# Six weight chunks rounded and split by DMAs, and one more projection in 512-wide pairs

## The chip, the cores and the metric

The kernel runs on one core of a Trainium2 chip. The metric is the device time of one execution in microseconds; the kernel before takes 251.93 us (median of three runs, 251.75 to 252.18). The engines are TensorE (PE for its matmuls, PEld for its weight loads), VectorE (DVE), ScalarE (ACT), GpSimd (POOL) and SyncE (SP). Each engine works through its own instructions in their order and waits on semaphores. SP issues almost all loads; in the kernel before, POOL issues none.

## The reference

Two decoder layers on x of 256 rows by 1024 (one batch). Each layer normalises x, projects it to 3584 columns, runs three branches over the pieces, gates them, and adds an output projection to x:

```python
hn = rms_norm(x, norm_gain)
proj = jnp.einsum('bsd,de->bse', hn, w_in)                      # 1024 -> 3584
a_q, a_k, a_v, a_g, b_x, b_g, c_q, c_k, c_v, c_g = jnp.split(proj, ...)
y_a = dilated_attention(rope(a_q), rope(a_k), a_v) * silu(a_g)  # 8 heads of 64
y_b = rg_lru_branch(b_x, ...) * silu(b_g)                       # 256 wide
y_c = stick_breaking_attention(c_q, c_k, c_v) * silu(c_g)       # 4 heads of 64
return x + jnp.einsum('bse,ed->bsd', concat(y_a, y_b, y_c), w_out)
```

A last RMSNorm follows the second layer. All inputs and the output are float32.

## The kernel before

**Precision.** Matmuls take float32r, a rounded float32. To keep float32 accuracy each operand is held twice: a rounded part `hi` and the rest `lo` = original - `hi`. A product is three matmuls: hi x hi, hi x lo and lo x hi. For the activations the parts are `xh` and `xl` (both in `xx`), or `yh` and `yl`.

**Weights** are packed in 18 chunks a layer, each 128 x 2048: 0 and 1 (`CH_AV`), 2 (`CH_CV`), 3 `CH_CQ`, 4 `CH_CK`, 5 and 8 `CH_AQ`, 6 and 9 `CH_AK`, 7 `CH_BX`, 10 `CH_CG` (C's gate), 11 `CH_BG`, 12 and 13 `CH_AG`, 14 to 17 the output projection. The second half of A's heads uses 8 and 9, called AQ1 and AK1 below; 5 and 6 are AQ0 and AK0. `load_chunk` (L101) fetches a chunk in two halves of 128 x 1024 into a staging tile `st` (five buffers) by a DMA on SP; ACT copies each 512 columns into `whi` (float32r, so the copy rounds), and DVE writes `wlo` = `st` - `whi`. `whi` and `wlo` have four buffers each, taken in rotation, so chunk n can be written only when TensorE is through with chunk n - 4. `ask` and `weights` (L117, L123) ask for a chunk two ahead of its use.

**A projection** of a 256-wide chunk is `proj_b` (L313), in two halves b = 0 and 1 of 128 columns. Unpaired (L340) a half is 24 matmuls 256 wide: `hi` with `xh`, `hi` with `xl`, `lo` with `xh`, eight k-blocks each, into half a PSUM bank. Paired (L323 to L338, chunks in `PAIRED[l]`) `hi` meets `xh` and `xl` at once: seven matmuls 512 wide, eight 256 wide for `lo`, and one more 512 wide, into one bank of its own for each half; ACT then copies the `xl` part out (`low`, L334) and DVE adds the two (L336, L338). Layer 0 pairs nothing; layer 1 pairs 3 to 9. Tag `pp` has three PSUM banks in rotation, so a half must wait until the bank of three before it has been read out.

**Order.** TensorE's order is the order in which the code is written. In a layer: V chunks, CQ, CK, AQ0 half 0, the stick-breaking scores (`sb_scores`, L434), AQ0 half 1, AK0, BX half 0, one block of transposes of the stick-breaking weights `sw` (`turned`, L460), BX half 1, two more blocks, AQ1 half 0, then `second` (the values `y` from the turned weights `wv`, L425, and A's first scores), AQ1 half 1, AK1, CG, transposes, BG half 0, `third` (gates, values, scores), BG half 1, AG, the output projection. The other engines' instructions are put in order by the framework's scheduler when the program is built. On ACT the sigmoids of `sb_scores` (L450, L451) feed DVE's scans (L456) and products (L458), whose result `sw` the transposes turn; ACT copies the turned blocks to `wv` (L466).

Of the kernel before, what the change touches and what calls it, by code (L numbers as in the profile page):

```python
# [9 lines left out]
F32 = mybir.dt.float32  # L10
F32R = mybir.dt.float32r
BF16 = mybir.dt.bfloat16
AF = mybir.ActivationFunctionType
ALU = mybir.AluOpType

P = 128
# [25 lines left out]

CH_AV, CH_CV, CH_CQ, CH_CK, CH_BX, CH_CG, CH_BG, CH_AG, CH_O = 0, 2, 3, 4, 7, 10, 11, 12, 14
CH_AQ, CH_AK = (5, 8), (6, 9)
PAIRED = ((), (CH_CQ, CH_CK, CH_AQ[0], CH_AK[0], CH_BX, CH_AQ[1], CH_AK[1]))


@with_exitstack
def trunk_kernel(ctx: ExitStack, tc: tile.TileContext, x, first_x, first, wpack, prm_d, gatew, gains, consts, rope, out):
    nc = tc.nc  # L50
    act, dve, pe, gps = nc.scalar, nc.vector, nc.tensor, nc.gpsimd
# [3 lines left out]
    wsp = ctx.enter_context(tc.tile_pool(name="wsp", bufs=4))  # L55
# [43 lines left out]
    split = {}  # L99

    def load_chunk(l, c):  # L101
        hi = wsp.tile([P, 2048], F32R, name="whi", tag="whi")
        lo = wsp.tile([P, 2048], F32R, name="wlo", tag="wlo")
        for i in range(2):
            st = wst.tile([P, 1024], F32, name="st", tag="st")
            nc.sync.dma_start(out=st, in_=wpack[l, c][:, i * 1024:(i + 1) * 1024])
            for j in range(0, 1024, 512):
                ws, ss = slice(i * 1024 + j, i * 1024 + j + 512), slice(j, j + 512)
                split[l, c] = act.activation(hi[:, ws], st[:, ss], AF.Copy)  # L109
                dve.tensor_sub(lo[:, ws], st[:, ss], hi[:, ws].bitcast(F32))  # L110
        return hi, lo
# [5 lines left out]
    def ask(l, c, ahead=AHEAD):  # L117
        last = order.index((l, c)) + ahead
        while pending and order.index(pending[0]) <= last:
            i = pending.pop(0)  # L120
            ready[i] = load_chunk(*i)

    def weights(l, c, ahead=AHEAD):  # L123
        ask(l, c, ahead)
        return ready.pop((l, c))
# [16 lines left out]
    for k in range(NK):  # L142
# [8 lines left out]
        hi, lo = [a[:, o:o + 768] for a in pair]  # L151
# [21 lines left out]
    prm_t = cst.tile([P, L * SM_P], F32, name="prm_t")  # L173
    nc.sync.dma_start(out=prm_t, in_=prm_d)
    ready[pending.pop(0)] = load_chunk(0, CH_CQ)
    xres = cst.tile([P, NT, D], F32, name="xres")
    for t in range(NT):
# [122 lines left out]
    for l in range(L):  # L300
# [12 lines left out]
        def proj_b(c, mid=None, to=None, sc=1.0):  # L313
            pair = c in PAIRED[l]
            hi, lo = [a.rearrange("p (k c) -> p k c", c=256) for a in weights(l, c, AHEAD - 1 if mid else AHEAD)]
            if pair:
                flat = None if to is not None else scr(512)
                to = v2(flat) if to is None else to
            else:
                flat = bank(pp, "pp")  # L320
            for b in range(2):
                cs = slice(b * P, b * P + P)
                if pair:  # L323
                    ps = bank(pp, "pp")
                    seq = [(0, k) for k in range(NK - 1)] + [(1, k) for k in range(NK)] + [(0, NK - 1)]
                    for i, (is_lo, k) in enumerate(seq):
                        if is_lo:
                            pe.matmul(ps[:, 0:S], lo[:, k, cs], xh[:, k, :], start=False, stop=False,  # L328
                                      skip_group_check=True)
                        else:  # L330
                            pe.matmul(ps, hi[:, k, cs], xx[:, k].rearrange("p h t -> p (h t)"), start=i == 0,  # L331
                                      stop=i == len(seq) - 1, skip_group_check=True)
                    low = wk.tile([P, S], F32, name="low", tag="low", bufs=2)
                    act.activation(low, ps[:, S:2 * S], AF.Copy, scale=sc)  # L334
                    if sc == 1.0:
                        dve.tensor_add(to[:, b, :], ps[:, 0:S], low)  # L336
                    else:
                        dve.scalar_tensor_tensor(to[:, b, :], ps[:, 0:S], sc, low, ALU.mult, ALU.add)  # L338
                else:
                    mm3(flat[:, b * 256:(b + 1) * 256], [lambda k, a=a: a[:, k, cs] for a in (hi, lo)],  # L340
                        [lambda k, a=a: a[:, k, :] for a in (xh, xl)], range(NK), True, True)
                if b == 0 and mid:
                    mid()
                    ask(l, c)
            return flat

        def proj_to(dst, c, mid=None, sc=1.0):
            if l > 0 and c in PAIRED[l]:
                proj_b(c, mid, dst, sc)
            else:  # L350
                scaled(dst, proj_b(c, mid), sc)
# [296 lines left out]
        for t in range(NT):  # L648
# [3 lines left out]
            for n2 in range(2):  # L652
                cs = slice(n2 * 512, n2 * 512 + 512)
# [5 lines left out]
                for c0, c1 in parts:  # L659
                    c = slice(n2 * 512 + c0, n2 * 512 + c1)  # L660
# [110 lines left out]
```

## Time and profile before

| | us |
|---|---|
| median of three runs (lowest, highest) | 251.93 (251.75, 252.18) |
| the profiled execution's own time | 251.52 |
| its span, first to last instruction | 249.4 |
| TensorE matmuls busy | 241.0 |
| DVE busy | 196.6 |
| ACT busy | 166.9 |
| POOL busy | 9.4 |
| read from HBM | 42.03 MB |

The span is what the profile's times are counted in; 2.1 us of the profiled execution lie around it. The granted TensorE clock was 0.997 over the span. A row of the timeline gives the start, the duration, the engine, the line, the operation and, in brackets, how long the engine sat idle before it and what released it; merged rows have a count. A row of the groups gives the count, the busy sum and the mean of one in ns, and the idle time before them. In the window rows the last three numbers are the granted clock, the busy share of the 16 DMA engines and the GB/s that they moved.

### The profile page before, as it was taken

The numbers are of one execution on the slowest core, as the hardware profiler recorded it, in microseconds if no ns is written. First come the engines' busy times: TensorE is split into PE (matmuls) and PEld (weight loads), VectorE is DVE, ScalarE is ACT, GpSimd is POOL, SyncE is SP. The second block draws the span as 40 slices with busy tenths as digits, with TensorE's granted clock in tenths as the row PEclk, the third lists the DMA queues.
The fourth block names the chain that finished last, engine by engine and source line by source line (L and its number), as shares of the span: only waits on it lengthen the run. The fifth ranks groups of instructions, "written<-read, shape, count | busy, mean of one in ns | idle before, by whom it ended". The sixth has DMA issues, their size and how long they took to land.

```text
span 249.4 us, 4520 instructions
## 1 busy us (share of the span) xinstructions
PE 241.0 (97%) x1657; PEld 214.7 (86%) x1657; DVE 196.6 (79%) x445; ACT 166.9 (67%) x360; POOL 9.4 (4%) x41
## 2 busy tenths in 40 slices
PE   8899999999999999999999999999999999999990
PEld 4689999998999799878889988888789979987870
DVE  3785499999999779996593666799999996985353
ACT  3667979933776599974672785775587649993142
POOL 0017200000000000000010000000000000000000
PEclk9999999999999999999999999999999999999998
DMA  6999988647536722277357378502542673000022
GB/s 177 382 271 407 352 284 292 257 132 226 179 110 231 265 78 93 85 218 257 116 160 260 119 263 279 182 4 84 174 166 89 222 254 114 0 0 3 0 84 84
DMA packets 13125, 43.36 MB, mean 174 GB/s; under 512 B 1584, under 2 KB 2224, under 8 KB 13104
## 3 DMA queue, kind: packets, MB, share of 16 engines
q1 hardware_dynamic: 12528, 42.30, 50.2%
q10 hardware_dynamic: 576, 0.79, 0.9%
q8 instruction: 13, 0.21, 0.3%
q14 instruction: 8, 0.07, 0.1%
HBM read 42.03 MB, written 1.05 MB: 173 GB/s over the span
## 4 chain that ended last, share of the span: by engine, by line
PE 94%; DMA 2%; DVE 1%; ACT 1%; SPq 0%; issue 0%; ACTq 0%
PE pp L214 50%; PE pp L331 10%; PE s L214 9%; PE pp L328 5%; PE s L169 4%; PE y L425 4%; PE s L465 3%; PE s L495 2%; DMA st<-first 2%; PE pp L169 2%; PE pp L545 1%; PE s L441 1%; PE s L262 1%; PE s L445 0%; DVE xres L661 0%; ACT scr L245 0%
## 5 line engine op out<-in xcount | busy, mean ns | idle before, releaser
L110 DVE TENSOR_TENSOR wlo<-st,whi 128x512 fp32r<-128x512 f32 x132 | 84.5, 686 | 14.7 <-ACT whi L109 14.4
L109 ACT ACTIVATE whi<-st 128x512 fp32r<-128x512 f32 x132 | 73.5, 627 | 24.6 <-PE pp L214 8.3
L214 PE MATMUL pp<-xx,whi 128*128 128x256 f32 x480 | 63.1, 284 | 0.0
L214 PEld LDWEIGHTS pp<-xx,whi 128*128 128x128 f32 x480 | 59.7, 191 | 1.0 <-issue 1.0
L214 PE MATMUL pp<-xx,wlo 128*128 128x256 f32 x240 | 33.7, 283 | 0.0
L214 PEld LDWEIGHTS pp<-xx,wlo 128*128 128x128 f32 x240 | 31.0, 192 | 0.0
L331 PE MATMUL pp<-xx,whi 128*128 128x512 f32 x112 | 29.3, 396 | 0.0
L331 PEld LDWEIGHTS pp<-xx,whi 128*128 128x128 f32 x112 | 20.1, 189 | 3.7 <-issue 0.3
L83 ACT ACTIVATE pr<-scr,mn 128x128 f32<-128x128 f32 (+1 forms) x32 | 14.1, 441 | 7.9 <-DVE mn L502 7.9
L77 ACT ACT_TABLE_LOAD x13 | 16.7, 1283 | 1.9 <-PEq L764 1.6
L328 PEld LDWEIGHTS pp<-xx,wlo 128*128 128x128 f32 x112 | 15.3, 190 | 1.1
L328 PE MATMUL pp<-xx,wlo 128*128 128x256 f32 x112 | 15.6, 282 | 0.0
L214 PE MATMUL pp<-whi,yh 128*128 128x512 f32 x48 | 14.1, 395 | 0.0
L214 PE MATMUL pp<-wlo,yh 128*128 128x512 f32 x48 | 13.9, 390 | 0.0
L214 PE MATMUL pp<-whi,yl 128*128 128x512 f32 x48 | 13.8, 390 | 0.0
L169 PE MATMUL s<-whi,xx 128*128 128x512 f32 (+1 forms) x36 | 10.3, 400 | 1.0 <-ACT xx L153 0.9
L466 ACT ACTIVATE wv<-s 128x512 f32<-128x512 f32 x18 | 9.6, 594 | 2.2 <-PE s L465 2.2
L334 ACT ACTIVATE low<-pp 128x256 f32<-128x256 f32 x14 | 5.3, 383 | 8.6 <-PE pp L331 8.6
L413 ACT ACTIVATE yh<-scr 128x512 fp32r<-128x512 f32 x8 | 5.1, 631 | 8.6 <-DVE scr L412 8.5
L214 PEld LDWEIGHTS pp<-wlo,yh 128*128 128x128 f32 x48 | 9.0, 188 | 1.9
L214 PEld LDWEIGHTS pp<-whi,yl 128*128 128x128 f32 x48 | 9.0, 188 | 1.9
L214 PEld LDWEIGHTS pp<-whi,yh 128*128 128x128 f32 x48 | 8.7, 188 | 1.6
(160 smaller groups left out, 353.2 us busy)
## 6 DMA issues: line engine op xcount, KB each, us to landing
st<-w_pack SPq DMA_DIRECT2D x66, 512.0 KB, 5.0
st<-first SPq DMA_DIRECT2D x7, 512.0 KB, 6.6
xres<-x_in SPq DMA_DIRECT2D x2, 512.0 KB, 8.5
gw_t<-gate_w SPq DMA_DIRECT2D x2, 256.0 KB, 6.6
gn<-gains SPq DMA_DIRECT2D x1, 512.0 KB, 7.3
gf<-gains SPq DMA_DIRECT2D x1, 512.0 KB, 4.9
out<-scr SPq DMA_DIRECT2D x2, 256.0 KB, 2.0
out<-scr ACTq DMA_DIRECT2D x2, 256.0 KB, 2.5
```

Of the source, the lines that this page charges most:

```text
L77: load = act.preload_act_table_set(name)
L83: i = dep(act.activation(*a, **k), loaded["load"])
L109: split[l, c] = act.activation(hi[:, ws], st[:, ss], AF.Copy)
L110: dve.tensor_sub(lo[:, ws], st[:, ss], hi[:, ws].bitcast(F32))
L169: pe.matmul(ps[t][:, c0 - base:c1 - base], a[:, k, t * P:(t + 1) * P], b[:, c0:c1], start=k == 0 and i == 0 and c0 == base, stop=k == NK - ...
L214: pe.matmul(ps, a(k), b(k), start=first and i == 0, stop=last and i == len(seq) - 1)
L328: pe.matmul(ps[:, 0:S], lo[:, k, cs], xh[:, k, :], start=False, stop=False, skip_group_check=True)
L331: pe.matmul(ps, hi[:, k, cs], xx[:, k].rearrange("p h t -> p (h t)"), start=i == 0, stop=i == len(seq) - 1, skip_group_check=True)
L334: act.activation(low, ps[:, S:2 * S], AF.Copy, scale=sc)
L425: pe.matmul(y[hr, p * 128 + o:p * 128 + 256], vt[:, s0, hs], wts[i][:, ws], start=s0 == 0, stop=s0 == 1)
L465: pe.transpose(tp[:, i * P:(i + 1) * P], tiles[h0 + h][:, j * P:(j + 1) * P], ident)
L466: act.activation(to[:, 4 * g:4 * g + 4, :].rearrange("p k c -> p (k c)"), tp, AF.Copy)
```

## The change

Chunks in a new table `SUMMED` take another way into `whi` and `wlo`: AQ1 and AK1 in layer 0; AQ1, AK1, CG and AG's first (12) in layer 1. For each half of such a chunk POOL issues a DMA from the packed weights straight into `whi` (float32 to float32r), ACT writes `wlo` = -`whi`, 1024 wide in one instruction, and POOL issues a second DMA of the same weights that adds to `wlo`. No `st` tile, no rounding copy on ACT and no subtraction on DVE is left for them. Besides, CG joins the paired chunks in layer 1.

```diff
+SUMMED = ((CH_AQ[1], CH_AK[1]), (CH_AQ[1], CH_AK[1], CH_CG, CH_AG))
-PAIRED = ((), (CH_CQ, CH_CK, CH_AQ[0], CH_AK[0], CH_BX, CH_AQ[1], CH_AK[1]))
+PAIRED = ((), (CH_CQ, CH_CK, CH_AQ[0], CH_AK[0], CH_BX, CH_AQ[1], CH_AK[1], CH_CG))
...
     def load_chunk(l, c):
+        if c in SUMMED[l]:
+            hi = wsp.tile([P, 2048], F32R, name="whi", tag="whi")
+            lo = wsp.tile([P, 2048], F32R, name="wlo", tag="wlo")
+            for i in range(2):
+                cs = slice(i * 1024, i * 1024 + 1024)
+                gps.dma_start(out=hi[:, cs], in_=wpack[l, c][:, cs])
+                split[l, c] = act.activation(lo[:, cs], hi[:, cs].bitcast(F32), AF.Copy, scale=-1.0)
+                gps.dma_start(out=lo[:, cs], in_=wpack[l, c][:, cs], accum_op=ALU.add)
+            return hi, lo
```

Below, lines of the changed kernel are ten higher than in the kernel before from `load_chunk`'s loop on (L334 is L344, L466 is L476). Three places show how instructions move.

On ACT in layer 1, ahead of the sigmoids of `sb_scores` (`scr<-s`), the kernel before has, with `low_1940` the copy of CK's second half, `low_1961` that of AQ0's first, and `whi_2061` the copies of AQ1's chunk:

```order
L334 ACTIVATE low_1940<-pp_1923 128x256
L109 ACTIVATE whi_2061<-st_2063 128x512 x2
L109 ACTIVATE whi_2061<-st_2069 128x512 x2
L334 ACTIVATE low_1961<-pp_1944 128x256
L83 ACTIVATE scr_1986<-s_1964 128x384
L83 ACTIVATE scr_1985<-s_1964 128x384
```

and the changed kernel, with `low_1928` and `low_1949` the same two halves:

```order
L344 ACTIVATE low_1928<-pp_1911 128x256
L344 ACTIVATE low_1949<-pp_1932 128x256
L109 ACTIVATE wlo_2050<-whi_2049 128x1024 x2
L84 ACTIVATE scr_1974<-s_1952 128x384
L84 ACTIVATE scr_1973<-s_1952 128x384
```

The rounding copies of AQ1 stood behind CK's copy; its negations (`wlo_2050`) now stand one row later, right ahead of the eight sigmoids, and each waits for the casting DMA of its half.

Further on, ACT has in the kernel before, from the copy of AK0's second half (`low_2113`) over those of BX's halves (`low_2141`, `low_2181`) to the last copy of the turned `sw` (`wv`), with `whi_2291` CG's chunk and `whi_2331` BG's:

```order
L334 ACTIVATE low_2113<-pp_2096 128x256
L109 ACTIVATE whi_2291<-st_2293 128x512 x2
L109 ACTIVATE whi_2291<-st_2299 128x512 x2
L334 ACTIVATE low_2141<-pp_2124 128x256
L466 ACTIVATE wv_2122<-s_2144 128x512
L334 ACTIVATE low_2181<-pp_2164 128x256
L109 ACTIVATE whi_2331<-st_2333 128x512
L466 ACTIVATE wv_2122<-s_2192 128x512
L466 ACTIVATE wv_2122<-s_2198 128x512
```

and the changed kernel, from AK0's first half (`low_2075`) on, with `low_2095` its second, and `low_2123` and `low_2157` those of BX:

```order
L344 ACTIVATE low_2075<-pp_2058 128x256
L109 ACTIVATE wlo_2133<-whi_2132 128x1024 x2
L344 ACTIVATE low_2095<-pp_2078 128x256
L344 ACTIVATE low_2123<-pp_2106 128x256
L476 ACTIVATE wv_2104<-s_2126 128x512
L109 ACTIVATE wlo_2268<-whi_2267 128x1024
L344 ACTIVATE low_2157<-pp_2140 128x256
L119 ACTIVATE whi_2301<-st_2303 128x512
L476 ACTIVATE wv_2104<-s_2168 128x512
L476 ACTIVATE wv_2104<-s_2174 128x512
```

AK1's negations (`wlo_2133`) stand ahead of the copies of AK0's second half and BX's first, and that of CG's first half (`wlo_2268`) ahead of two of the three `wv` copies.

On POOL the kernel before has no DMA; the changed one has in layer 1, behind the clears of `sw` and two small scalars:

```order
L108 DMA whi_2049<-w_pack 128x1024 x2
L110 DMA wlo_2050<-w_pack 128x1024 x2
L108 DMA whi_2132<-w_pack 128x1024 x2
L110 DMA wlo_2133<-w_pack 128x1024
L108 DMA whi_2267<-w_pack 128x1024
L110 DMA wlo_2133<-w_pack 128x1024
L108 DMA whi_2267<-w_pack 128x1024
L110 DMA wlo_2268<-w_pack 128x1024 x2
```

Rows `whi` are casting DMAs and rows `wlo` adding ones: 2049 and 2050 are AQ1, 2132 and 2133 AK1, 2267 and 2268 CG. A casting DMA waits until TensorE is through with the chunk four before (CK, AQ0 and AK0 in turn), an adding one for ACT's negation of its half, and all that stands behind on POOL waits with it. AG's four follow. In layer 0 the four casting DMAs of AQ1 and AK1 stand together, and the four adding ones behind them.

On TensorE only C's gate in layer 1 changes: its two unpaired halves (48 matmuls 256 wide) become two paired ones (16 of 512 and 16 of 256), between AK1's last half and the transposes of A's weights. On DVE the subtractions of the six chunks are gone, and in layer 1 the addition for AQ0's second half (L336) stands ahead of the last of the four `sw` products, no longer behind it.

## Prediction

> **What bounds the kernel now.** I read the page's busy line and its chain first, then TensorE's timeline over the span, then the stages that the change touches on each engine.
>
> ```profile
> PE 241.0 (97%) x1657; PEld 214.7 (86%) x1657; DVE 196.6 (79%) x445; ACT 166.9 (67%) x360; POOL 9.4 (4%) x41
> ...
> PE 94%; DMA 2%; DVE 1%; ACT 1%; SPq 0%; issue 0%; ACTq 0%
> ...
> L110 DVE TENSOR_TENSOR wlo<-st,whi 128x512 fp32r<-128x512 f32 x132 | 84.5, 686 | 14.7 <-ACT whi L109 14.4
> L109 ACT ACTIVATE whi<-st 128x512 fp32r<-128x512 f32 x132 | 73.5, 627 | 24.6 <-PE pp L214 8.3
> ```
>
> TensorE is busy 97% of the span, and 94% of the chain that ended last is its own work. The splitting of weights on ACT (L109) and DVE (L110) is the largest group of each, yet appears in no share of the chain that matters. Do weights ever come late? The rows of TensorE's timeline that show an idle time before them are these two, over the whole span:
>
> ```profile
> 1.17 3.17 PE L140 MATMUL y<-cold 128*128 128x512 bf16 x7 [1.17 <-DVE cold L128]
> ...
> 8.21 0.71 PE L169 MATMUL s<-whi,xx 128*128 128x512 f32 x2 [0.94 <-ACT xx L153]
> ```
>
> Both lie in the first 9 us, before any chunk of the change. So relieving ACT and DVE, by itself, buys nothing: TensorE's own rows set the end, and the change can gain only where it takes rows from TensorE.
>
> **The gain on TensorE.** The rows of AK1's last halves, of C's gate, and of what follows it:
>
> ```profile
> 183.16 2.00 PE L331 MATMUL pp<-xx,whi 128*128 128x512 f32 x8
> 185.95 2.00 PE L331 MATMUL pp<-xx,whi 128*128 128x512 f32 x8
> 188.98 2.08 PE L214 MATMUL pp<-xx,whi 128*128 128x256 f32 x16
> 191.86 2.08 PE L214 MATMUL pp<-xx,whi 128*128 128x256 f32 x16
> 194.74 1.47 PE L465 MATMUL s<-con,pr 128*128 128x128 f32 x12
> ```
>
> C's gate takes 194.74 - 188.98 = 5.76 us unpaired. A paired half takes 185.95 - 183.16 = 2.79, two of them 5.58. The gain is **0.18 us**, 0.07% of 251.52, and nothing else leaves TensorE. What C's gate now adds (two `low` copies, two additions) lies beside other matmuls.
>
> **What leaves ACT and DVE, and what comes.** Six chunks by four: 24 of the 132 subtractions (84.5/132 = 0.64 us each, 15.4 us) leave DVE, 24 copies (73.5/132 = 0.56, 13.4 us) leave ACT, and 12 negations come. A copy 1024 wide is not in the trace; the 768-wide row below and L109's 627 ns at 512 give 204 ns for 256 columns, so 831 + 204 = 1.03 us, 12.4 us in all. All that is off the chain and costs nothing as busy time. What counts is where these negations wait.
>
> ```profile
> L159 ACT ACTIVATE whi<-st 128x768 fp32r<-128x768 f32 x6 | 5.0, 831 | 0.0
> L106 SPq DMA_DIRECT2D st<-w_pack x66: 327/328/597, 12.5 to 208.2; - x66
> DMA to landing us min/median/max: 3.6/5.0/9.3
> st<-w_pack SPq DMA_DIRECT2D x2, 512.0 KB, 4.4
> 35.00:40.00 5.00, 5.00 (x48) 4.49 (x48) 5.00 (x10) 3.55 (x6) 0.00 (x0) 1.00 0.91 320
> 161.00:167.00 6.00, 6.00 (x37) 5.33 (x36) 5.82 (x14) 5.34 (x11) 0.00 (x0) 1.00 0.10 38
> ```
>
> **Price of the new DMAs.** None like them is in the trace. The nearest rows are the 512 KB loads on SP: 3.6 us from issue to landing at best, 9.3 at worst, and 4.4 in the window 154 to 162 us, where the first pair of layer 1 would run. At 320 GB/s and a share of 0.91 the engines move 352 GB/s when full, so 1.5 us of a load is data and the best one has 2.1 us besides. I take 4.4 for a casting DMA (its place is the same) and 1.5 for each that follows directly. An adding DMA has to read its target too, so I take 3.0 us of data; from below 1.5 (as a load). From above nothing bounds it but the worst landing, 9.3. POOL's own time for issuing one is not in the trace; SP's is 0.33 us, and up to 1.5 us it hides behind the data of the DMA before, so I take 0. Total traffic is not the issue: 12 loads give way to 24 (6.3 MB more), and between 161 and 167 us the engines are at a share of 0.10.
>
> **Layer 0.** The rows of TensorE at the end of CK and where AQ1 needs its rest, and the sigmoids on ACT:
>
> ```profile
> 34.34 1.12 PE L214 MATMUL pp<-xx,wlo 128*128 128x256 f32 x8
> 57.91 1.12 PE L214 MATMUL pp<-xx,wlo 128*128 128x256 f32 x8
> 40.66 3.13 ACT L83 ACTIVATE scr<-s 128x384 f32<-128x384 f32 x8
> ```
>
> AQ1's slot is free at about 34.4, its casts land by 34.4 + 4.4 + 1.5 = 40.3, ACT negates behind the sigmoids, 43.7 to 45.8, and the adding DMAs land by about 45.8 + 2.1 + 2 x 3.0 + AK1's casts 2 x 1.5 = 56.9 at the latest. TensorE needs them at 57.9. I take 0; the cover is 1 us, and each microsecond beyond it costs one.
>
> **Layer 1, the term that decides.** The rows of TensorE first, then ACT's, then DVE's:
>
> ```profile
> 154.20 2.00 PE L331 MATMUL pp<-xx,whi 128*128 128x512 f32 x8
> 167.49 2.00 PE L331 MATMUL pp<-xx,whi 128*128 128x512 f32 x8
> 174.55 1.88 PE L331 MATMUL pp<-xx,whi 128*128 128x512 f32 x7
> 177.53 1.52 PE L425 MATMUL y<-wv,vc 128*64 128x256 f32 x16
> 154.63 0.39 ACT L334 ACTIVATE low<-pp 128x256 f32<-128x256 f32 x1 [2.41 <-PE pp L331]
> 159.15 3.17 ACT L83 ACTIVATE scr<-s 128x384 f32<-128x384 f32 x8 [1.34 <-PE s L445]
> 163.63 0.39 ACT L334 ACTIVATE low<-pp 128x256 f32<-128x256 f32 x1
> 174.76 1.08 ACT L466 ACTIVATE wv<-s 128x512 f32<-128x512 f32 x2
> 159.67 1.00 DVE L456 TENSOR_TENSOR_SCAN sw<-scr,zero 128x127 f32<-128x127 f32 x2 [1.27 <-ACT scr L83]
> 165.14 0.56 DVE L458 TENSOR_TENSOR sw<-scr,sw 128x384 f32<-128x384 f32 x1
> 165.62 0.42 DVE L336 TENSOR_TENSOR scr<-pp,low 128x256 f32<-128x256 f32 x1
> ```
>
> Rows of eight at L331 hold one matmul of the half that ends and seven of the next. CK ends at 154.4; ACT sees it at 154.6, and POOL can then issue AQ1's casts.
>
> *Step 1.* The halves land at 154.6 + 4.4 = 159.0 and 160.5. ACT negates to 160.0 and 161.5. The eight sigmoids stand behind, so they start at **161.5**, not 159.15. DVE's scans follow them, and the addition that frees the PSUM bank of AQ0's second half stands behind the scans. It ends at 165.62 + 0.42 = 166.04 in the trace, 6.9 us after the first sigmoid; the change puts it ahead of the last product (0.5 us), so 6.4: 167.9. BX's first half takes that bank at 167.49 + 0.23 = 167.7. TensorE loses **0.2 us**.
>
> *Step 2.* AQ1's adding DMAs go out at 160.0 and 161.5, AK1's casts right behind them on POOL; I take it that the engines serve them in that order. Data from 160.0 + 2.1 = 162.1: two of 3.0, then a cast of 1.5, so AK1's first half lands at 169.6. Its negation ends at 170.6 (ACT itself is there from about 166.7: the copy of AK0's first half ends 4.9 us after the sigmoids start, and one `low` more now stands ahead of it). AK0's second half is copied after the other negation, by about 172.5; AQ1 needs its bank at 174.55. No loss.
>
> *Step 3.* AK1's first adding DMA goes out at 170.6, and only behind it CG's first cast. Data from 172.7: 3.0 and 1.5, landed at **177.2**; negated at 178.2. Behind it on ACT stand the copy of BX's second half (0.3), one of BG (0.56), and then the second `wv` block, done at about 179.6. The values at 177.53 (177.7 after step 1) need it: TensorE loses **1.9 us**. Before, it was there at 175.3.
>
> From there on all moves together: AK1's, CG's and AG's rests are needed 8 us and more after their negations. Sum: 0.2 + 1.9 - 0.18 = **+1.9 us**: 253.4 against the profiled execution's 251.52, and 253.8 against the median, 0.41 above it. That is the number predicted.
>
> **The rule of the Trainium skill on this.** The page "DMA: Bandwidth & Descriptors", in "Anatomy of one DMA — SWDGE (gpsimd) path", fits 2.0 us plus the bytes at 436 GB/s to a DMA issued from GpSimd; for 512 KB that is an estimate of 3.2 us, below this trace's best row of 3.6. By it step 1 loses nothing, and with adding DMAs at twice the bytes step 3 ends with CG's cast at 173.4 and no loss: 251.75, the first rival. The same page, in "Two DMAs through the same engine are not ordered", says that descriptors of one queue on one engine start in order, which speaks for the order that step 2 takes and against the hidden case by free sharing; no run here shows either yet.
>
> **Rivals.**
>
> *All hidden, no slower.* The place is CG's first cast, and it decides at a landing of 175.1 (177.5 less 1.03, 0.3, 0.56 and 0.54). If an adding DMA costs the engines 1.5 us, as a plain load, AK1's first half lands at 166.6, is negated by 167.7, CG's cast lands at 172.8, and ACT then waits for BX's matmuls as before. That gives 251.93 - 0.18 + 0.2 = 251.95, or 251.75 with casts at 3.6 us. For it: the engines are nearly idle there (0.10). Against it: three round trips POOL, DMA, ACT have to fit between 154.6 and 175.1, with an order on ACT in which one late cast holds back sigmoids or `wv`. It decides at about 2.1 us for each adding DMA. A cast that is not held up by the adding DMAs ahead of it (161.5 + 4.4 + 1.03 = 166.9 for AK1's first negation) would hide everything in the same way.
>
> *Adding or casting far slower.* With 6.0 us of data for an adding DMA, AK1's first half lands at 175.6 and CG's at 186.2; the `wv` block is done at about 188.6 and TensorE has lost 11 us: 263. With all three casts landing in 6.0 instead of 4.4, it is three times 1.6 more: 258.6. The worst landing of the trace, 9.3, in all three would add three times 4.9, 268.5; it comes from engines that many loads share, which is not so here.
>
> *Faster by more than the gate's 0.18.* It would need a stall of TensorE that the lighter ACT and DVE remove. The timeline shows none after the first 9 us, and those of the start and the end are untouched.
>
> *The parts are not what they say* (the casting DMA does not round, say): the result would differ, not the time.
>
> **How the numbers follow.** The forecast's case (0.5 to 4 us lost behind CG's cast) has 0.42, the far slower one 0.19, all hidden 0.35, faster 0.04. A change within 0.2% (0.5 us) can't be told from none here. So faster 0.04, same 0.35, slower 0.61. The range reaches down to the hidden case, 251.6, and up to the case of three slow casts, 258.5; beyond are some 0.1 of the far slower cases and most of the faster one.
>
> **What would show it.** Right: in the list of waits ACT waiting for a DMA into `whi` at L109, largest ahead of the sigmoids and ahead of the second `wv`; TensorE waiting for ACT `wv` at the values of layer 1 (L435) and, less, for DVE at BX. C's gate at 5.6 us. Wrong: TensorE without a wait after the start (then the adding DMAs are cheap); waits for DMA at L341 or L338 (then the rests come late, not the negations); or a loss in layer 0.

## The result, and the profile after

| | before | changed |
|---|---|---|
| median, the runs shown with this result (lowest, highest), us | 251.84 (251.46, 252.18) | 258.68 (258.47, 259.37) |
| ratio, 95% interval | | 1.0277 [1.0252, 1.0301] |
| span of the profiled execution, us | 249.4 | 256.7 |

The changed kernel is 6.8 us slower. The forecast was 253.8, 1.9 us slower, and its range ended at 258.5. Here and below a ratio is taken from the executions in the chip's faster state alone and a median from all of them, so the two can differ a little. The page of the changed kernel, its busy line, its row of granted clock and its chain:

```profile
PE 243.2 (95%) x1641; PEld 214.9 (84%) x1641; DVE 184.8 (72%) x423; ACT 166.6 (65%) x350; POOL 27.0 (11%) x65
...
PEclk9999999999999999999999999999799999999998
...
PE 83%; issue 6%; DMA 5%; POOL 2%; ACT 1%; DVE 1%; SPq 0%; POOLq 0%; ACTq 0%
...
L109 ACT ACTIVATE wlo<-whi 128x1024 fp32r<-128x1024 f32 x12 | 12.8, 1067 | 21.5 <-DMA whi<-w_pack 21.4
```

The subtractions left DVE as forecast: that group fell from 84.5 to 68.9 us, and DVE from 196.6 to 184.8 us busy in all. TensorE's share of the chain fell from 94% to 83%, and DMA and POOL have come into it. ACT sat idle 21.4 us in all ahead of negations, waiting for casting DMAs. One slice of TensorE's clock, the one from 179.7 to 186.1 us, is at 7 tenths.

Where TensorE waits for that, by its timeline in layer 1 (the columns are start, duration, engine, line, operation, idle time before it and releaser):

```profile
168.12 1.89 PE L341 MATMUL pp<-xx,whi 128*128 128x512 f32 x7 [0.98 <-DVE scr L346]
...
178.04 0.65 PE L435 MATMUL y<-wv,vc 128*64 128x256 f32 x2
183.48 2.82 PE L435 MATMUL y<-wv,vc 128*64 128x256 f32 x14 [4.79 <-ACT wv L476]
186.23 1.76 PE L505 MATMUL s<-k,q 64*128 64x128 f32 x16
187.91 1.88 PE L341 MATMUL pp<-xx,whi 128*128 128x512 f32 x7
```

These are the two places that were forecast: BX's bank, 0.98 us and not 0.2, and the second `wv` block at the values, 4.79 us and not 1.9. Something else stands here too. From the restart at 183.48 to the next projection the values and scores take 187.91 - 183.48 = 4.43 us. The windows over this stretch say why (behind the length stand the busy times of PE, PEld, DVE, ACT and POOL; granted clock, busy share of the DMA engines and GB/s are the last three numbers):

```profile
180.00:183.00 3.00, 0.00 (x0) 0.00 (x0) 0.51 (x2) 1.91 (x4) 0.55 (x1) 1.00 1.08 246
183.00:184.00 1.00, 0.52 (x5) 0.52 (x7) 1.00 (x3) 0.91 (x2) 0.41 (x1) 0.60 0.93 344
184.00:185.00 1.00, 1.00 (x9) 0.81 (x7) 0.93 (x3) 0.14 (x1) 0.00 (x0) 0.50 1.00 90
185.00:186.00 1.00, 1.00 (x8) 0.51 (x4) 0.36 (x1) 1.00 (x2) 0.00 (x0) 0.50 0.89 160
186.00:187.00 1.00, 1.00 (x10) 0.75 (x10) 0.53 (x1) 1.00 (x3) 0.78 (x1) 0.69 1.04 205
187.00:188.00 1.00, 1.00 (x13) 0.64 (x9) 1.00 (x3) 0.74 (x2) 0.09 (x1) 1.00 0.69 131
```

From about 183.2 to 186.6 us, 3.4 us, TensorE is granted half its clock. Where the wait comes from, on ACT and on POOL:

```profile
153.89 0.39 ACT L344 ACTIVATE low<-pp 128x256 f32<-128x256 f32 x1 [2.41 <-PE pp L341]
159.69 1.06 ACT L109 ACTIVATE wlo<-whi 128x1024 fp32r<-128x1024 f32 x1 [2.63 <-DMA whi<-w_pack]
171.23 1.06 ACT L109 ACTIVATE wlo<-whi 128x1024 fp32r<-128x1024 f32 x1 [4.20 <-DMA whi<-w_pack]
181.09 1.06 ACT L109 ACTIVATE wlo<-whi 128x1024 fp32r<-128x1024 f32 x1 [6.52 <-DMA whi<-w_pack]
182.84 1.07 ACT L476 ACTIVATE wv<-s 128x512 f32<-128x512 f32 x2
```

```profile
172.59 0.89 POOL L110 DMA_DIRECT2D wlo<-w_pack  x1 [8.32 <-ACT wlo L109]
173.15 0.89 POOL L108 DMA_DIRECT2D whi<-w_pack  x1
173.84 1.09 POOL L110 DMA_DIRECT2D wlo<-w_pack  x1
174.39 1.10 POOL L108 DMA_DIRECT2D whi<-w_pack  x1
```

The three ACT rows at L109 are the first negations of AQ1, AK1 and CG; the last one holds back the `wv` copies, which start at 182.84. CG's first cast, issued at 173.15, has AK1's first adding DMA ahead of it; AK1's second one follows 0.7 us behind it, and CG's second cast 1.2 us. The DMA view over 173.0 to 173.6 us (size and time from issue to landing):

```profile
wlo<-w_pack POOLq DMA_DIRECT2D x1, 512.0 KB, 5.4
whi<-w_pack POOLq DMA_DIRECT2D x1, 512.0 KB, 7.9
```

The adding DMA landed at 172.59 + 5.4 = 178.0, the cast at 173.15 + 7.9 = 181.05, three microseconds later. SP issues no load between 158 and 185 us in this kernel, so the engines carry only POOL's own DMAs then.

### The profile page after: what moved, and what is told of

Read it like the earlier page. It is cut to its first block, busy times and chain, and to the rows that moved or that the text cites. A ratio compares the mean times of both kernels' runs of the same rounds, so it can differ in the third digit from the quotient of the medians.

```text
span 256.7 us, 4479 instructions
## 1 busy us (share of the span) xinstructions
PE 243.2 (95%) x1641; PEld 214.9 (84%) x1641; DVE 184.8 (72%) x423; ACT 166.6 (65%) x350; POOL 27.0 (11%) x65
## 4 chain that ended last, share of the span: by engine, by line
PE 83%; issue 6%; DMA 5%; POOL 2%; ACT 1%; DVE 1%; SPq 0%; POOLq 0%; ACTq 0%
PE pp L224 47%; PE s L224 9%; PE pp L341 7%; PE y L435 4%; PE s L179 4%; PE pp L338 3%; DMA whi<-w_pack 3%; PE s L475 3%; PE s L505 2%; DMA st<-first 2%; PE pp L179 2%; PE pp L555 1%; POOL wlo L110 1%; POOL whi L108 1%; PE s L272 1%
## 5 line engine op out<-in xcount | busy, mean ns | idle before, releaser
L120 DVE TENSOR_TENSOR wlo<-st,whi 128x512 fp32r<-128x512 f32 x108 | 68.9, 685 | 18.0 <-ACT whi L119 17.9
L119 ACT ACTIVATE whi<-st 128x512 fp32r<-128x512 f32 x108 | 60.2, 623 | 19.6 <-PE s L224 6.4
L224 PE MATMUL pp<-xx,whi 128*128 128x256 f32 x448 | 59.0, 284 | 0.0
L224 PEld LDWEIGHTS pp<-xx,whi 128*128 128x128 f32 x448 | 55.6, 192 | 1.0 <-issue 1.0
L341 PE MATMUL pp<-xx,whi 128*128 128x512 f32 x128 | 33.6, 396 | 1.0 <-DVE scr L346 1.0
L341 PEld LDWEIGHTS pp<-xx,whi 128*128 128x128 f32 x128 | 23.0, 189 | 5.5 <-DVE scr L346 1.3
L109 ACT ACTIVATE wlo<-whi 128x1024 fp32r<-128x1024 f32 x12 | 12.8, 1067 | 21.5 <-DMA whi<-w_pack 21.4
L110 POOL DMA_DIRECT2D wlo<-w_pack x12 | 10.8, 902 | 37.2 <-ACT wlo L109 30.0
L224 PE MATMUL pp<-wlo,yh 128*128 128x512 f32 x48 | 13.8, 390 | 0.0
L224 PE MATMUL pp<-whi,yl 128*128 128x512 f32 x48 | 13.8, 389 | 0.0
L108 POOL DMA_DIRECT2D whi<-w_pack x12 | 8.1, 690 | 48.4 <-PE pp L341 33.5
L466 DVE TENSOR_TENSOR_SCAN sw<-scr,zero 128x127 f32<-128x127 f32 (+1 forms) x16 | 8.0, 541 | 5.1 <-ACT scr L84 5.1
L476 ACT ACTIVATE wv<-s 128x512 f32<-128x512 f32 x18 | 9.6, 593 | 1.5 <-PE s L475 1.5
```

The costliest lines, as they stand in the source:

```text
L108: gps.dma_start(out=hi[:, cs], in_=wpack[l, c][:, cs])
L109: split[l, c] = act.activation(lo[:, cs], hi[:, cs].bitcast(F32), AF.Copy, scale=-1.0)
L110: gps.dma_start(out=lo[:, cs], in_=wpack[l, c][:, cs], accum_op=ALU.add)
L224: pe.matmul(ps, a(k), b(k), start=first and i == 0, stop=last and i == len(seq) - 1)
```

## The experiments

The kernel before took 250.72 us beside the first four runs, 251.67 beside the next four and 251.62 beside the last four. Each ratio is to the kernel before on the same chip.

**One part alone.** C's gate paired, nothing through the new DMAs:

```diff
-SUMMED = ((CH_AQ[1], CH_AK[1]), (CH_AQ[1], CH_AK[1], CH_CG, CH_AG))
+SUMMED = ((), ())
```

> C's gate in 512-wide pairs as in the change, but no chunk takes the new way through DMAs. Main theory: the pairing is only the 0.18 us that its rows show (5.76 to 5.58), so 251.84 - 0.18 = about 251.65, with no wait on TensorE after the first 9 us. Rival: the pairing itself (two PSUM banks more in rotation, two copies and additions more) makes a wait near C's gate or the gate of B behind it, then at or above 251.84.

Measured: 251.37 us, ratio 1.0033 [1.0014, 1.0051]. It is the rival. TensorE, and DVE's product that reads bank `y`, in this run:

```profile
200.54 0.68 DVE L422 TENSOR_TENSOR scr<-y,cg 128x512 f32<-128x512 f32 x1
201.37 1.52 PE L435 MATMUL y<-wv,va 128*64 128x256 f32 x16 [0.86 <-DVE scr L422]
```

and the same product in the kernel before:

```profile
199.39 0.70 DVE L412 TENSOR_TENSOR scr<-y,cg 128x512 f32<-128x512 f32 x1
```

The gate's result now passes through a copy and an addition before its sigmoid; the product comes 1.15 us later, and `y` has one buffer only. 0.86 - 0.18 = 0.68 us is the loss, and the medians give 0.65.

Layer 0's AQ1 and AK1 alone:

```diff
-SUMMED = ((CH_AQ[1], CH_AK[1]), (CH_AQ[1], CH_AK[1], CH_CG, CH_AG))
+SUMMED = ((CH_AQ[1], CH_AK[1]), ())
-PAIRED = ((), (CH_CQ, CH_CK, CH_AQ[0], CH_AK[0], CH_BX, CH_AQ[1], CH_AK[1], CH_CG))
+PAIRED = ((), (CH_CQ, CH_CK, CH_AQ[0], CH_AK[0], CH_BX, CH_AQ[1], CH_AK[1]))
```

> Only layer 0's AQ1 and AK1 go through the new DMAs; layer 1 and C's gate as before. Main theory: nothing is lost in layer 0, 251.84 within 0.3. Rival: part of the 6.8 us that the change costs comes from layer 0 (its TensorE shows no wait there, but a start or a table load could move), then 252.3 or more.

Measured: 250.41 us, ratio 0.9986 [0.9971, 1.0001]: no loss, and no gain that can be told from none. Its one wait after the start shows that the cover was used up to the last:

```profile
57.89 0.74 PE L224 MATMUL pp<-xx,wlo 128*128 128x256 f32 x4 [0.26 <-DMA wlo<-w_pack]
```

All but CG through the new DMAs:

```diff
-SUMMED = ((CH_AQ[1], CH_AK[1]), (CH_AQ[1], CH_AK[1], CH_CG, CH_AG))
+SUMMED = ((CH_AQ[1], CH_AK[1]), (CH_AQ[1], CH_AK[1], CH_AG))
```

> As the changed kernel, but C's gate loads its chunk the old way (still paired); AQ1, AK1 and AG keep the new way in layer 1. Theory A (the third link of the chain through POOL, the DMAs and ACT: CG's first negation stands ahead of the wv copies on ACT): the 4.79 us wait at the values and the low clock behind it go, the 0.98 us at BX stays: 251.84 - 0.18 + 0.98 = about 252.6. Theory B (the adding DMAs keep the engines so busy that AK1's rests, or the negations of AK1 themselves, come too late whatever CG does): 2 us or more of waits remain, at the values or at AK1's wlo, 254.5 or more.

Measured: 253.32 us, ratio 1.0094 [1.0060, 1.0129]. The wait at the values is gone, as theory A says. The total is not theory A's. On this chip the kernel before is 1.1 us faster, so its 252.6 is 251.5 here and theory B's bound of 254.5 is 253.4: the total is nearer to B, though the waits are not where B put them. Besides BX (0.95 us) a second bank comes late, ahead of C's gate:

```profile
170.35 1.06 ACT L109 ACTIVATE wlo<-whi 128x1024 fp32r<-128x1024 f32 x1 [3.70 <-DMA whi<-w_pack]
...
172.96 0.43 DVE L346 TENSOR_TENSOR scr<-pp,low 128x256 f32<-128x256 f32 x1 [2.04 <-ACT low L344]
...
190.25 1.89 PE L341 MATMUL pp<-xx,whi 128*128 128x512 f32 x7 [0.99 <-DVE scr L346]
```

The first two rows show where this may come from: AK1's negations hold a `low` copy on ACT, and DVE sits idle for it. That DVE is still late at 190.25 because of this is a reading of one trace and was not tried by itself. So CG's casts are what holds the values, but what is left of the change in layer 1 is not free either.

**The clock.** The fillers ahead of the values:

```diff
             y = bank(yp, "y")
+            if l == 1 and h0 == 0 and vt is vc:
+                for i in range(18):
+                    pe.matmul(y, xh[:, 0, 0:P], xx[:, 0].rearrange("p h t -> p (h t)"), start=True, stop=True,
+                              skip_group_check=True)
```

> The changed kernel with 18 matmuls of 512 columns (about 0.25 us each, 4.5 us) ahead of the values of layer 1, into the bank that the values then overwrite, so that TensorE is busy while it waits for the turned weights. Theory: the clock of 0.5 behind the 4.8 us wait comes from the idle time; filled, the clock stays at 1.0 and the values take 1.5 us and not 2.8: about 1.5 to 2 us less, 256.7 to 257.2. Rival: the clock falls there for another reason, or the wait alone makes the loss: 258.7 or, if the fillers delay the values, up to 259.5.

Measured: 256.74 us, ratio 1.0250 [1.0223, 1.0278]. This is below the changed kernel's 1.0277 by 0.7 us, where 1.5 to 2 were expected, and the intervals overlap; the trace is clearer.

```profile
177.41 4.26 PE L433 MATMUL y<-xx 128*128 128x512 f32 x18
181.60 2.17 PE L439 MATMUL y<-wv,vc 128*64 128x256 f32 x16
...
185.22 1.88 PE L341 MATMUL pp<-xx,whi 128*128 128x512 f32 x7
...
181.62 1.07 ACT L480 ACTIVATE wv<-s 128x512 f32<-128x512 f32 x2
...
183.00:186.00 3.00, 3.00 (x28) 2.19 (x24) 1.88 (x5) 2.41 (x5) 0.87 (x1) 1.00 0.89 156
...
206.26 1.52 PE L439 MATMUL y<-wv,va 128*64 128x256 f32 x16 [0.88 <-DVE scr L422]
```

The fillers end just as the second `wv` copy starts. From there to the next projection it takes 185.22 - 181.62 = 3.60 us; in the changed kernel 187.91 - 182.84 = 5.07. The clock stays at 1.00 while TensorE is kept busy. So in these two executions 1.47 us of the loss is the low clock that comes with the idle time, and not the wait itself. Not all of it comes back in the total: the last row is a wait at the third branch that the changed kernel does not have.

**What makes the casts late.** Only the first half of each chunk through the new DMAs:

```diff
+            nc.sync.dma_start(out=st, in_=wpack[l, c][:, 1024:2048])
+            for j in range(0, 1024, 512):
...
+                split[l, c] = act.activation(hi[:, ws], st[:, ss], AF.Copy)
+                dve.tensor_sub(lo[:, ws], st[:, ss], hi[:, ws].bitcast(F32))
-            for i in range(2):
+            for i in range(1):
                 cs = slice(i * 1024, i * 1024 + 1024)
                 gps.dma_start(out=hi[:, cs], in_=wpack[l, c][:, cs])
```

> As the changed kernel, but only the first half of each of the six chunks goes through the new DMAs, the second half the old way. So each casting DMA goes out alone, with no second one right behind it. Theory (a DMA that follows directly shares the engines with the first and delays its landing, it does not queue behind it): AQ1's lone cast in layer 1 lands 4.4 to 4.8 us after issue, not 5.5; the sigmoids start about 2 us earlier, the wait at BX goes, and the wait at the values falls from 4.8 to 0.5 to 1.5 us: 251.5 to 252.5 on a chip where the kernel before takes 250.7. Rival (a cast of 512 KB takes 5.5 us whatever stands beside it): AQ1's lone cast lands at 5.5 as before, and BX still waits 0.5 us or more.

Measured: 252.75 us (250.86 to 253.91), ratio 1.0038 [1.0013, 1.0063]. The profiled execution is the fastest of the ten and shows no wait after the start, neither at BX nor at the values; the slower ones have no trace, so where they wait is not known. In it AQ1's lone cast landed 4.1 us after issue. CG's landed 6.1 us after issue, with one adding DMA ahead of it and no DMA of POOL behind, 1.3 us after that one (168.86 + 6.1 against 168.31 + 5.4). SP issued a load at 170.77, behind CG's cast, but by the DMA view its packets begin at 174 us only; up to there the engines move POOL's alone.

Without the adding DMAs, so that the rests of these chunks are left out of the result:

```diff
-                gps.dma_start(out=lo[:, cs], in_=wpack[l, c][:, cs], accum_op=ALU.add)
```

> As the changed kernel without the adding DMAs: wlo stays the negated rounded weights in the six chunks, so the rests are left out of the result there. The twelve casts, the negations and ACT's order stay. Theory (two adding DMAs of about 2.6 us of engine time each stand ahead of AK1's and CG's casts): without them AK1's casts land 5.5 to 6 us after issue as AQ1's did, not 8.4, CG's likewise, the wait at the values goes to under 1 us, the one at BX (0.98) stays: 251.3 to 252.3. Rival (the casts themselves, or the round trip through POOL and ACT, make the delay): 3 us or more of the wait at the values stay, 255 or more.

Measured: 251.97 us, ratio 1.0005 [0.9984, 1.0027]. The wait at the values is gone, that at BX stays (0.95). By the DMA view AK1's first cast, issued at 162.82 with its second 0.5 us behind it, lands 4.0 us after issue, and CG's first, likewise followed, 4.1; AQ1's lone one in the run before took 4.1. So a cast that follows a cast takes nothing from it here. The line of POOL's queue in the page (packets, MB, share of 16 engines' span) gives the price of both kinds; first this run, then the changed kernel:

```profile
q0 software_dynamic: 1728, 6.29, 7.9%
```

```profile
q0 software_dynamic: 3456, 12.58, 21.3%
```

The packets of 12 casts took 0.079 x 250.6 = 19.8 us of all 16 engines, 1.65 each. In the changed kernel it is 0.213 x 256.7 = 54.7 us, so 34.9 for 12 adding DMAs, 2.9 each, if a cast costs the same in both.

All DMAs kept, the adding ones behind the casts of the next chunk (`flush(cast)` issues those of the chunk before, held in `later`, behind the cast given):

```diff
-                gps.dma_start(out=lo[:, cs], in_=wpack[l, c][:, cs], accum_op=ALU.add)
+            flush(cast)
...
+                later.append((lo[:, cs], wpack[l, c][:, cs]))
```

> As the changed kernel, all DMAs kept, but on POOL the adding DMAs of a chunk stand behind the casting DMAs of the next one: AQ1's casts, AK1's casts, AQ1's adding ones, CG's casts, AK1's and CG's adding ones. ACT's order is nearly unchanged; CG's two negations still stand ahead of two wv copies. Theory (the order on POOL, with casts held behind adding DMAs that wait for negations, makes the wait at the values; the traffic as such does not): the wait at the values goes or is under 0.5 us, BX keeps its 1 us: 251.3 to 252.0. Rival (the engines' occupancy): the casts share the engines with adding DMAs anyway and CG's land 8 us and more after issue; 2 us or more of the wait stay, 254 or more.

Measured: 253.23 us, ratio 1.0052 [1.0031, 1.0073]. The wait at the values is gone with the same DMAs. CG's casts go out at 168.56 and not at 173.15, since nothing that waits for AK1's negations stands ahead of them any more:

```profile
164.00 1.84 POOL L106 DMA_DIRECT2D wlo<-w_pack  x2
168.56 1.10 POOL L116 DMA_DIRECT2D whi<-w_pack  x2 [2.71 <-PE pp L353]
...
203.21 1.52 PE L447 MATMUL y<-wv,va 128*64 128x256 f32 x16 [0.76 <-DVE scr L434]
```

They still take 7.6 us to land. What is left is 0.93 us at BX and the pairing's wait at the third branch, 0.76. The wait at BX also helps: it brings TensorE to the values 0.93 us later.

The negations on POOL:

```diff
-                split[l, c] = act.activation(lo[:, cs], hi[:, cs].bitcast(F32), AF.Copy, scale=-1.0)
+                gps.tensor_scalar(lo[:, cs], hi[:, cs].bitcast(F32), -1.0, None, ALU.mult)
```

> As the changed kernel, but the negations stand on POOL and not on ACT, so that nothing on ACT waits for a casting DMA: neither the sigmoids nor the wv copies. The chain of DMAs is as long as before, or longer, since POOL holds its queue while it negates. Theory (the loss is only what stands behind the negations on ACT, the rests themselves are in time): no wait at BX nor at the values; the gate's 0.18 us remains as a gain, less up to 1 us where DVE's new order holds a bank: 250.5 to 251.5. Rival (the rests come late too, or POOL's negation is several us long): waits of TensorE for wlo at the paired halves, 252.5 or more.

Measured: 271.8 us, ratio 1.0779 [1.0753, 1.0805]: the rival, and far beyond it. A negation takes POOL nearly three times as long as ACT (median 3.08 us, against 1.07), and the DMAs queue behind it:

```profile
168.27 2.98 POOL L109 TENSOR_SCALAR wlo<-whi 128x1024 fp32r<-128x1024 f32 x1 [4.21 <-DMA whi<-w_pack]
...
73.19 1.22 PE L224 MATMUL pp<-xx,wlo 128*128 128x256 f32 x4 [5.69 <-DMA wlo<-w_pack]
...
210.20 0.74 PE L338 MATMUL pp<-xx,wlo 128*128 128x256 f32 x4 [2.44 <-DMA wlo<-w_pack]
```

TensorE waits for rests here, four times, 13.8 us in all, and its clock falls to 0.50 around three of them.

**The changed kernel again, as the measure of the last three runs.**

> The changed kernel itself once more, on the chip of the next three runs, as their measure: 1.024 to 1.030 of the kernel before, waits of about 1.0 us at BX and 4.3 to 4.8 us at the values, the granted clock at 0.5 for some 3 us behind the second.

Measured: 259.0 us, ratio 1.0286 [1.0253, 1.0319]; 4.97 us of wait at the values, the same low clock. BX did not wait this time, which was not expected: AQ1's first negation began 4.7 us after CK's copy and not 5.8. The total is still the same: CK's copy came 0.87 us later in this execution, so that CG's first negation starts at the same time in both.

```profile
154.76 0.39 ACT L344 ACTIVATE low<-pp 128x256 f32<-128x256 f32 x1 [2.41 <-PE pp L341]
159.50 1.06 ACT L109 ACTIVATE wlo<-whi 128x1024 fp32r<-128x1024 f32 x1 [1.57 <-DMA whi<-w_pack]
171.53 1.06 ACT L109 ACTIVATE wlo<-whi 128x1024 fp32r<-128x1024 f32 x1 [4.69 <-DMA whi<-w_pack]
181.08 1.06 ACT L109 ACTIVATE wlo<-whi 128x1024 fp32r<-128x1024 f32 x1 [6.22 <-DMA whi<-w_pack]
```

**What stands behind a DMA.** AK1's second adding DMA and CG's second cast held until CG's first half is negated:

```diff
+                if (l, c, i) == (1, CH_CG, 1):
+                    dep(cast, held["behind"])
...
+                if (l, c, i) == (1, CH_AK[1], 1):
+                    held["out"], held["in"] = lo[:, cs], wpack[l, c][:, cs]
+                    continue
+                if (l, c, i) == (1, CH_CG, 0):
+                    seen = wk.tile([P, 1], F32, name="seen", tag="seen", bufs=1)
+                    held["behind"] = gps.tensor_scalar(seen, lo[:, 0:1].bitcast(F32), 1.0, None, ALU.mult)
+                    dep(gps.dma_start(out=held["out"], in_=held["in"], accum_op=ALU.add), held["behind"])
```

> As the changed kernel, but on POOL AK1's second adding DMA and CG's second casting DMA go out only when CG's first half has landed and been negated, so that nothing stands behind CG's first casting DMA while it is under way; what stands ahead of it is unchanged. Theory (a DMA issued later shares the engines with one under way and delays its landing): CG's first cast lands 6.1 us after its issue, as where half of each chunk took the new way, and not 7.9; the wait at the values falls by about 1.8 us to 3.0, and the total by 1.8 to 2.5. Rival (first come, first served on the engines; the cast is late because of what stands ahead of it): 7.9 again, the same wait at the values, the total unchanged or more, since the DMAs held back come later.

Measured: 261.89 us, ratio 1.0410 [1.0384, 1.0436]. On the disputed point the theory holds, in one execution each: CG's first cast lands 6.3 us after issue (7.6 in the changed kernel beside it), and the wait at the values falls from 4.97 to 2.85. On the total it fails:

```profile
173.16 0.88 POOL L123 DMA_DIRECT2D wlo<-w_pack  x1 [8.00 <-ACT wlo L113]
173.72 0.88 POOL L109 DMA_DIRECT2D whi<-w_pack  x1
181.19 0.23 POOL L119 TENSOR_SCALAR seen<-wlo 128x1 f32<-128x1 f32 x1 [6.59 <-ACT wlo L113]
...
182.42 2.20 PE L448 MATMUL y<-wv,vc 128*64 128x256 f32 x14 [2.85 <-ACT wv L489]
197.31 1.88 PE L354 MATMUL pp<-xx,whi 128*128 128x512 f32 x7 [1.65 <-DVE scr L359]
211.41 1.52 PE L448 MATMUL y<-wv,va 128*64 128x256 f32 x16 [1.97 <-DVE scr L435]
...
190.52 1.06 ACT L113 ACTIVATE wlo<-whi 128x1024 fp32r<-128x1024 f32 x1 [5.84 <-DMA whi<-w_pack]
```

CG's second negation now comes at 190.5, where ACT stands idle for it for 5.84 us, and TensorE waits twice later on, for DVE. The same pattern has moved on to the next thing in ACT's queue.

**Versions that might beat both.** AG alone through the new DMAs, CG paired:

```diff
-SUMMED = ((CH_AQ[1], CH_AK[1]), (CH_AQ[1], CH_AK[1], CH_CG, CH_AG))
+SUMMED = ((), (CH_AG,))
```

> C's gate paired, and of the six chunks only layer 1's AG through the new DMAs. Theory: the 0.86 us that the pairing alone lost at the third branch's values (DVE late with the product that frees the bank y) goes, because four subtractions of 0.6 us leave DVE near there, and AG's casts, asked for 10 us ahead of any wv copy, hold back nothing that TensorE waits for: 0.2 us below the kernel before. Rival: the wait of DVE's product is set by ACT or by CG's own additions, and 0.5 us or more of it stay: 0.3 to 0.7 us above the kernel before.

Measured: 252.31 us, ratio 1.0017 [0.9996, 1.0038]: the rival's case by the trace, since 0.96 us of wait for DVE's product stays at the third branch's values. Four subtractions less on DVE do not bring it forward.

Casts first, and AQ1's negations behind the sigmoids:

```diff
+                if (l, c) == (1, CH_AQ[1]):
+                    dep(split[l, c], loaded["users"][-1])
```

> All six chunks through the new DMAs, with the casting DMAs ahead of the adding ones as in the run with that order, and AQ1's two negations in layer 1 put behind the eight sigmoids on ACT. Theory (the 1 us at BX is only the sigmoids held behind AQ1's negations): no wait at BX and none at the values of layer 1; what is left is the gate's gain of 0.18 us and up to 0.8 us of wait at the third branch's values: from 0.2 us below to 0.7 us above the kernel before. Rival: the adding DMAs, 4 to 5 us later now, bring the rests of AQ1 too late: TensorE waits for a DMA into wlo at AQ1's halves (L338's place), 1.5 us or more above the kernel before.

Measured: 252.95 us, ratio 1.0060 [1.0040, 1.0080]. BX no longer waits, as said; but 0.92 us of wait is back at the values, because CG's negations ran from 175.42 to 177.66 on ACT, ahead of two `wv` copies. In the run with casts first the wait at BX had hidden this lateness. With the 0.76 us at the third branch and the gate's 0.18 that makes 1.5 us, which is what the ratio gives, and above the theory's 0.7. No version beat the kernel before by an amount that can be told from none.

## Why the prediction was right or wrong

**Right: what bounds the kernel, and what the relief of ACT and DVE is worth.** With 11.8 us less on DVE, no run gained beyond the uncertainty.

**Right as rows, wrong as cover: the gate.** Its paired halves take 5.58 us and not 5.76. But "What C's gate now adds lies beside other matmuls" fails when the gate stands alone (0.86 us of wait). In the changed kernel 0 to 0.25 us of wait is left at that place, in the two executions with a profile; TensorE comes there 7 us later.

**Right: the price of the data.** 1.5 us for a cast and 3.0 for an adding DMA were taken; 1.65 and 2.9 were measured. Layer 0 costs nothing, but not by the forecast's working: with SP's loads beside them its first casts landed 7.6 and 9.4 us after issue (changed kernel, layer 0 alone) and not 4.4, and the cover of 1 us was used up. That nothing was lost there is in part luck.

**Right: the place and the mechanism.** Step 1 and step 3 name BX's bank and the second `wv` copy, and both are there. Step 2 as well: AK1's late cast costs nothing at once, though the run without CG's casts shows DVE held by it.

**Wrong: the size of step 3, and from it of the sum.** The step that failed is the chain through POOL, the DMAs and ACT, which was sized too short, its last link most: 7.6 us where 9.6 to 9.9 were measured. Step 2 says "I take it that the engines serve them in that order", and the prediction counted for each cast only what stands ahead of it; POOL's own time it put at 0. The links of the chain, from the start of CK's copy on ACT over the starts of the three first negations:

| from, to | predicted | changed kernel | again |
|---|---|---|---|
| CK's copy to AQ1 | 4.4 | 5.8 | 4.7 |
| AQ1 to AK1 | 10.6 | 11.5 | 12.0 |
| AK1 to CG | 7.6 | 9.9 | 9.6 |
| sum | 22.6 | 27.2 | 26.3 |

The last link is 2.0 to 2.3 us too short. In the held run, with nothing behind CG's first cast, it took 180.04 - 171.80 = 8.2 us, so 1.3 to 1.6 us come from the adding DMA and the cast that follow; the cast's own landing fell from 7.6 to 6.3. In the run with half of each chunk, with no DMA of POOL behind it, it landed at 168.86 + 6.1 = 174.96, where the prediction's own figures (2.1, 3.0 and 1.5 us after 168.31) give 174.9. So DMAs issued later on POOL can delay one under way, and that is shown for these two together. It is not so for any DMA: a cast behind a cast cost nothing (4.0 and 4.1 us), and SP's load began only as CG's cast ended. Which of the two DMAs does it, the adding one perhaps, was not tried. Of the other 0.6 us of the last link, 0.4 stands ahead of POOL's issue, which came 1.36 us after the negation began (171.80 to 173.16) and not 1.0; the rest is open.

The Trainium skill's page "DMA: Bandwidth & Descriptors", section "Two DMAs through the same engine are not ordered", was cited for the order assumed; it says that descriptors start in order but are pipelined. The delay seen here fits the pipelined half, which the working left out, but no run here shows the descriptors themselves.

The first link varied, 4.7 and 5.8 in two executions of one kernel; why is open, and a second cast right behind the first does not explain it. Of the second link's excess of 0.9 to 1.4 us, 0.4 is again the time from the negation's start to POOL's issue; the rest was not tried by itself. That CG's negation holds the values by its place on ACT is shown by leaving CG out and by letting its casts go first; putting the negation behind the `wv` copies on ACT was not tried.

**Missing: the clock.** "From there on all moves together" left out that TensorE slows down once it has been idle; 1.47 us by the traces with and without the fillers, 0.7 by the ratios. The Trainium skill's page "TensorE: Matmul & The Clock Gate", section "Why this matters for your kernels", advises against idle gaps above about 3 us; the 4.8 us here agree with it, though two shorter gaps in the list below had the same effect.

**The sum.** By the spans, 256.7 - 249.4 = 7.3 us. From the values' start to the next projection stood 180.49 - 177.53 = 2.96 us before and 187.91 - 178.04 = 9.87 now, 6.9 more: 4.79 idle, 1.5 of clock, and 0.6 more around the break that is not booked as idle. BX adds 0.98, the gate takes 0.18, and the first 9 us were 0.7 shorter in the profiled execution (its first wait for ACT is 0.25 us and not 0.94; in the other execution of the same kernel it is 1.38). 0.3 us is left unexplained.

**Of the rivals.** "Adding or casting far slower" gave 258.6 for three slow casts, close to the time measured, but not for its reason: the price of the data was as forecast, and the casts were late by company. "All hidden" fell where it was said to decide: CG's cast landed at 181.05, its limit was 175.1. "A cast that is not held up by the adding DMAs ahead of it" was not seen; without any adding DMA it all but came true (1.0005). The bound of 2.1 us for each adding DMA, at which the hidden case ends, is a slip: its own terms give 2.3 (168.2 + 3 x 2.3 = 175.1), which at 2.9 changes nothing.

## What to carry to other kernels

An asynchronous transfer whose landing an in-order engine waits for delays everything queued behind that wait; here an ACT queue that had slack in busy time lost most of 6.8 us to one negation put ahead of copies that TensorE needed. When several DMAs are issued on one queue within a microsecond or two, price the landing of each by what is issued behind it as well (1.3 us here, for an adding DMA and a cast), and put the ones that somebody waits for first: that order alone brought the loss from 2.8% to 0.5%. Count a stall of TensorE of several microseconds as longer than it looks, since its clock falls with it (1.47 us here on a wait of 4.79).

## What was not expected of the hardware

- **The clock falls after gaps of under 3 us too.** Gaps of 2.85 us (the held run, ahead of 182.42) and 2.44 us (negations on POOL, ahead of 210.20) were followed by 3.4 us at 0.50, as the one of 4.79 us; gaps of 0.99, 1.65 and 1.97 us were not. In the held run the clock was still 1.00 when TensorE went on, and fell 0.7 us later, for 183.1 to 186.5:

```profile
183.00:184.00 1.00, 1.00 (x10) 0.62 (x7) 0.96 (x3) 1.00 (x3) 0.85 (x1) 0.55 0.63 74
184.00:186.00 2.00, 2.00 (x12) 1.50 (x12) 2.00 (x5) 0.69 (x2) 0.00 (x0) 0.50 1.05 207
```

- **The low clock comes in lengths of 3.4 us.** Narrow windows place it at 183.2 to 186.6 in the changed kernel and, with the negations on POOL, at 71.2 to 78.0, 197.5 to 204.3 and 211.1 to 214.6: 3.4, 6.8, 6.8 and 3.4 us. Three of these begin within a gap and one 0.9 us behind it. Whether it matters where in such a rhythm a gap falls was not tried.
- **An adding DMA of 512 KB into float32r takes 2.9 us of the 16 engines, a casting one 1.65.** The adding one landed 5.4 us after issue, with nothing else ahead of it.
- **POOL needs 3.08 us (median of 12) to negate 128 x 1024 float32; ACT needs 1.07 (mean of 12).**
